# Splitting weights into two parts: the low part by an accumulating transfer, three units ahead, 64-byte tile offsets

## The chip, the cores and the metric

The kernel runs on one core of a Trainium2 chip. The metric is the time of one execution on the device in microseconds (us), the lower the better; a figure for a kernel is the median of its runs. The core has TensorE (PE, its weight loads PEld), VectorE (DVE), ScalarE (ACT), GpSimd (POOL) and the sync engine (SP, which here only issues DMAs), all in order, each with its own instruction stream, and 16 DMA engines that all queues share.

## The reference, cut to what matters

A decoder trunk of two layers on 512 tokens of width 1024, all in float32. Layer 0 mixes tokens by a chunked spatial gate, layer 1 by an attention with forget gates; a gated MLP with a short causal convolution follows each.

```python
for i in range(DEPTH):                      # DEPTH = 2
    hn = rmsnorm(h, mix_norm_g[i])
    mix = gating(hn, w_in, ..., w_out)      # i = 0: (u * s) @ w_out
          attention(hn, w_qkvf, b_f, w_o)   # i = 1: 16 heads of 64
    h = h + mix
    hn = rmsnorm(h, ffn_norm_g[i])
    h = h + (silu(conv3(hn @ w_gate)) * (hn @ w_up)) @ w_down
return rmsnorm(h, final_norm_g)
```

Nearly all the work is in the products with weights: 23 million weights, 92 MB.

## The kernel before

Every float32 product is made of three. Each operand is split into a high part, rounded to the format that TensorE multiplies at full rate (float32r), and a low part, the exact rest; `triple` (L164) then issues high by high, high by low and low by high (L167 to L169) into one bank of PSUM.

The weights lie in memory as 176 units of 128 rows by 1024 float32 (512 KB). `unit` (L85) hands out the next unit, and lets `fetch` (L75) prepare one more behind it: a DMA on SP's queue into a tile `raw` (three of them), a cast on ACT to `whi` (L112), and a subtraction on DVE, raw minus whi, to `wlo` (L113). There are two tiles each of `whi` and `wlo`, so the cast of a unit waits until TensorE has read the unit two before it. One unit feeds 8 blocks, 24 matmuls of 128 by 128 by 512. `fetch` makes 171 units so; unit 0 is split in two halves by `split` in `build`, and the last four are split into tiles `x` in `last_down`.

The stages, in order, with the units that each uses: the v half of the gate (16, tokens stationary, `gemm_tm`), its u half (16, weights stationary, `gemm_fm`, with the mixing of chunks between), its output product (16), gate and up of MLP 0 (32, eight groups of four units, with the convolution and silu after each group), down (16), the attention's values (8), queries and keys (16, the heads' work woven between), its output (8), gate and up of MLP 1 (32), and the last down product (16, tokens stationary). In the four output and down products the activations are the tiles `z` (32 of them); in the others they are the tiles `x` (16).

After an output product `add_to_h` (L211) adds the residual on DVE, makes the next `x` on ACT and DVE, and squares on ACT; `norm_square` (L132) adds the squares up on POOL (L141). Beside these 28 additions POOL has the constants of the start and 16 copies in the attention.

A scheduler decides the order in which each engine's instructions stand, from the program's order and its own estimate of when each is ready. Tiles get their place in a partition of SBUF in the order in which their names first come up, one behind the other: `raw`, `whi`, `wlo`, `x`, `tmp` come before `mv` (statistics of the gate, 4 by 2 float32, 32 bytes); `R`, `pt`, `tc`, `z` and `hl` come after it.

At the start (L673 to L705) TensorE warms up with 9 small matmuls on `ones`; unit 0 and the first quarter of the activations are loaded in halves, unit 1 is fetched between the rest of `x`.

Of the kernel before, what the change touches and what calls it, by code (L numbers as in the profile page):

```python
# [8 lines left out]
F32 = mybir.dt.float32  # L9
F32R = mybir.dt.float32r  # L10
BF16 = mybir.dt.bfloat16
I32 = mybir.dt.int32
AF = mybir.ActivationFunctionType
# [3 lines left out]
P = 128  # L17
T = 512            # tokens
D = 1024
KD = D // P        # feature tiles of the model width  # L20
E = 2048           # gMLP width and FFN width
KE = E // P
G = 8              # spatial groups
NT = T // P        # token tiles
H = 16             # heads
# [4 lines left out]
LAG = 7            # blocks between the logits and the sums of values  # L30

# columns of the packed per-feature vectors
V_MIX = 0          # mix_norm_g, 2 layers x 8 tiles
V_FFN = 16         # ffn_norm_g, 2 x 8
V_CW = 32          # conv taps, 2 x 3 x 16
V_CB = 128         # conv bias, 2 x 16
V_LG = 160         # ln_g, 16
V_LB = 176         # ln_b, 16
NV = 192
NU = 176           # units of weights  # L40


class Trunk:
# [31 lines left out]
    def fetch(self):  # L75
        nc = self.nc
        raw = self.sb("raw", 3, [P, 1024])
        nc.sync.dma_start(out=raw, in_=self.ins["w"][self.iu])
        self.iu += 1
        hi = self.sb("whi", 2, [P, 1024], F32R)  # L80
        lo = self.sb("wlo", 2, [P, 1024], F32R)
        self.split(hi, lo, raw)
        self.ahead.append((hi, lo))

    def unit(self):  # L85
        """The next unit of weights, in two parts; the one after it is under way."""
        while len(self.ahead) < 2 and self.iu < NU - 4:
            self.fetch()
        return self.ahead.pop(0)

# [1 line left out]
    def rsqrt(self, src, n, scale, eps):  # L92
        """[P, n] -> 1/sqrt(src*scale + eps): a first guess from the exponent, then Newton."""
        nc = self.nc
        ms, y, t = self.small(n), self.small(n), self.small(n)
        nc.vector.tensor_scalar(out=ms, in0=src, scalar1=scale, scalar2=eps, op0=ALU.mult, op1=ALU.add)
        nc.vector.tensor_scalar(out=y.bitcast(I32), in0=ms.bitcast(I32), scalar1=-0.5, scalar2=float(0x5F3759DF),
                                op0=ALU.mult, op1=ALU.add)
        for _ in range(3):
            self.newton(y, ms, t)  # L100
        return y

    def newton(self, y, ms, t):
        """y towards 1/sqrt(ms)."""
        nc = self.nc
        nc.vector.tensor_tensor(out=t, in0=y, in1=y, op=ALU.mult)
        nc.vector.scalar_tensor_tensor(out=t, in0=t, scalar=-0.5, in1=ms, op0=ALU.mult, op1=ALU.mult)
        nc.vector.scalar_tensor_tensor(out=y, in0=t, scalar=1.5, in1=y, op0=ALU.add, op1=ALU.mult)
# [6 lines left out]
    def norm_split(self, k, gcol, parts=1):  # L115
        """Operand parts of h*g for feature tile k."""
        nc = self.nc
        if k == 0:
            self.acc, self.xh, self.xl = None, [], []
        h = self.h[k]  # L120
        g = self.vec[:, gcol + k : gcol + k + 1]
        xh = self.sb("x", 16, [P, T], F32R)
        xl = self.sb("x", 16, [P, T], F32R)
        for q in range(parts):
            c = slice(q * T // parts, (q + 1) * T // parts)
            nc.scalar.activation(out=xh[:, c], in_=h[:, c], func=AF.Copy, scale=g)
            nc.vector.scalar_tensor_tensor(out=xl[:, c], in0=h[:, c], scalar=g, in1=xh[:, c].bitcast(F32),
                                           op0=ALU.mult, op1=ALU.subtract)
        self.xh.append(xh)
        self.xl.append(xl)  # L130

    def norm_square(self, k):  # L132
        """Feature tile k's share of the sum of squares."""
        nc = self.nc
        if self.acc is None:
            self.acc = self.tmp()
            nc.scalar.activation(out=self.acc, in_=self.h[k], func=AF.Square)
        else:
            sq = self.tmp()
            nc.scalar.activation(out=sq, in_=self.h[k], func=AF.Square)  # L140
            nc.gpsimd.tensor_tensor(out=self.acc, in0=self.acc, in1=sq, op=ALU.add)  # L141

    def norm_end(self):
        """r4[:, i]: 1/rms of token i*128+p.  R: the same along the free axis, on every partition."""
        nc = self.nc
        pt = self.ps("a")
        for i in range(NT):
            nc.tensor.matmul(pt[:, i : i + 1], self.acc[:, i * P : (i + 1) * P], self.ones[:, 0:1], start=True, stop=True)
        self.r4 = self.rsqrt(pt[:, 0:NT], NT, 1.0 / D, RMS_EPS)
        dg = self.tmp()  # L150
        for i in range(NT):
            nc.vector.tensor_scalar(out=dg[:, i * P : (i + 1) * P], in0=self.ident, scalar1=self.r4[:, i : i + 1],
                                    scalar2=None, op0=ALU.mult)
        self.dg = dg
# [9 lines left out]
    def triple(self, out, a, b, start, stop):  # L164
        """a*b to float32's accuracy from the exact parts of a and b."""
# [5 lines left out]
    def gemm_fm(self, o, nk, groups, evac, each=None, banks0=None):  # L171
        """Feature-major: four 128-feature tiles a group, weights stationary.  Yields after every 128x128 block."""
# [15 lines left out]
    def gemm_tm(self, o, nk, groups, evac, each=None):  # L188
        """Token-major: four token tiles a group of 512 features, tokens stationary."""
# [21 lines left out]
    def add_to_h(self, gcol):  # L211
        """Evacuation of an output product: the residual, then the next norm's operand."""
# [10 lines left out]
    def gmlp(self):  # L223
# [3 lines left out]
        mv = self.sb("mv", 1, [P, NT, 2])  # L227
# [38 lines left out]
        def mix(c):  # L266
            """The mixed chunks of feature tile c, with the norm's scale and shift and the spatial bias."""
# [42 lines left out]
    def spatial(self):  # L310
        """Causal spatial weights, transposed: [s, g, t], with their sums over s on every partition."""
# [46 lines left out]
    def fox(self):  # L358
# [4 lines left out]
        # the parts of the gates' weights side by side  # L363
# [44 lines left out]
        # Blocks of products fill the tensor engine's waits in the attention: logits of one head beside  # L408
        # the transposes and sums of the one before it.
# [20 lines left out]
    def gates(self):  # L430
        """Logs of the forget gates, [token, head]."""
# [14 lines left out]
        # log sigmoid z = min(z, 0) - log(1 + e^-|z|);  log(1 + e^-|z|) = 2 atanh s,  s = (1 - th)/(3 + th),  th = tanh(|z|/2)  # L446
# [15 lines left out]
    def running_sums(self):  # L462
        """Running sums of the logs, [head, token], in two parts, and negated: four rows a head beside the parts of
        q and of k: cum, cum, 1, 1 and 1, 1, -cum, -cum."""
# [29 lines left out]
    def stack_q(self, p, pq, st):  # L494
        """Operands of the logits of heads 2p and 2p+1: the parts of q and k, stacked along the contraction."""
# [22 lines left out]
    def attend(self, slot):  # L518
        """Logits of one block; some blocks behind them the transposes, and behind those the sums of values."""
# [9 lines left out]
    OFF = (0, 128, 384, 768)   # where the rows of a query block begin in a head's tile of probabilities  # L529

    def logits(self, h, qi):
        """Softmax's numerators of query block qi, and the diagonal of its normalizers' inverses."""
# [18 lines left out]
    def turn(self, h, kb):  # L551
        """Probabilities of key block kb, transposed and normalized, in two parts."""
# [8 lines left out]
        hl = self.sb("hl", 3, [P, 1024], F32R)  # L561
# [27 lines left out]
    def last_down(self):  # L589
        """Token-major down projection with the residual, then the final norm."""  # L590
# [13 lines left out]
        def finish(i, parts):  # L604
            # 1/rms from a square root and one step of Newton's
# [18 lines left out]
        for g in range(2):  # L624
            # a token tile's columns, in two parts where the norm of the last tile waits for them
# [22 lines left out]
        # the last quarter token tile by token tile, so that only the last tile's norm is left at the end  # L648
        last = []
        for kp in range(half, KE // 2):  # L650
            raw = self.sb("raw", 3, [P, 1024])
# [13 lines left out]
    def build(self):  # L665
        nc, tc = self.nc, self.tc
        with tc.tile_pool(name="sb", bufs=1) as self.pool, \
# [3 lines left out]
            # the activation table and the tensor engine's clock get ready while the first loads run  # L671
# [9 lines left out]
            raw = self.sb("raw", 3, [P, 1024])  # L681
            hi, lo = self.sb("whi", 2, [P, 1024], F32R), self.sb("wlo", 2, [P, 1024], F32R)
# [53 lines left out]
def blocks(w):  # L736
    """[K, 512*n] -> units of two 128-row tiles by 512 columns, group by group."""
# [5 lines left out]
def qk_blocks(w):  # L743
    """q and k columns of a pair of heads beside each other, four 128-row tiles a unit."""
# [49 lines left out]
```

## Time and profile before

| | us |
|---|---|
| three runs | 1111.95, 1113.28, 1115.22 |
| median | 1113.28 |
| span of the profiled execution | 1110.7 |
| TensorE busy in it | 1098.0 (99%) |
| DVE, ACT, POOL busy | 618.5, 443.5, 66.4 |
| granted TensorE clock, mean | 0.998 |

The profile is one execution on the chip, its times counted from the span's start. The median of the runs is 2.57 us above the profiled span. A matmul's recorded time overlaps that of its neighbours, since they are pipelined; its pace is read from the distance of two starts, or from how often a unit's buffers are released.

### The profile page before, as it was taken

Reading aid. Unit: us, or ns where it says so; the run is one execution under the profiler, and the core shown is the slowest. Engines: PE = TensorE matmul, PEld = TensorE weight load, DVE = VectorE, ACT = ScalarE, POOL = GpSimd, SP = SyncE. Lnnn points to the kernel's source line nnn. Section 1 sums busy time; section 2 is a strip of 40 time slices with the busy share of each in tenths; the row PEclk is TensorE's granted clock in tenths of the full one; section 3 lists DMA queues with packets and bytes.
Section 4 is the critical chain, followed back from the end, with each engine's and each line's share of the span. In section 5 each row is a group of like instructions: output and inputs, shape, how many; then the busy total and the mean of one; then the engine's idle time right before and its main releaser. Section 6 shows DMA issues by size and latency. Waiting matters only on the chain. (4 is left out here: it accounts for less than half of the span.)

```text
span 1110.7 us, 13297 instructions
## 1 busy us (share of the span) xinstructions
PE 1098.0 (99%) x5210; PEld 905.7 (82%) x5210; DVE 618.5 (56%) x1007; ACT 443.5 (40%) x706; POOL 66.4 (6%) x62
## 2 busy tenths in 40 slices
PE   8999999999999999999999999999999999999997
PEld 6878888888888888888888788888878888888886
DVE  6435765533556655624264688888665656644232
ACT  5332333332334333423142566776542434332222
POOL 6000000000200000001020000000021000000000
PEclk9999999999999999999999999999999999999999
DMA  7322222223222222222222212111122222222222
GB/s 245 103 78 98 91 76 95 76 95 95 95 95 95 94 95 95 95 96 94 95 95 82 79 40 62 58 40 58 62 90 95 95 96 95 95 95 94 96 77 76
DMA packets 28959, 99.47 MB, mean 90 GB/s; under 512 B 3488, under 2 KB 4256, under 8 KB 28896
## 3 DMA queue, kind: packets, MB, share of 16 engines
q1 hardware_dynamic: 28752, 98.52, 26.9%
q8 instruction: 41, 0.67, 0.2%
q14 instruction: 22, 0.18, 0.1%
q10 hardware_dynamic: 144, 0.10, 0.0%
HBM read 96.12 MB, written 2.10 MB: 88 GB/s over the span
## 5 line engine op out<-in xcount | busy, mean ns | idle before, releaser
L113 DVE TENSOR_TENSOR wlo<-raw,whi 128x1024 fp32r<-128x1024 f32 (+1 forms) x173 | 218.8, 1266 | 389.8 <-ACT whi L112 377.4
L112 ACT CAST whi<-raw 128x1024 fp32r<-128x1024 f32 (+1 forms) x173 | 180.7, 1045 | 467.0 <-PE psg L168 124.2
L167 PE MATMUL psg<-x,whi 128*128 128x512 f32 x336 | 136.7, 407 | 0.0
L169 PE MATMUL psg<-x,wlo 128*128 128x512 f32 x336 | 131.3, 391 | 0.0
L168 PE MATMUL psg<-x,whi 128*128 128x512 f32 x336 | 130.8, 389 | 0.0
L167 PE MATMUL pss<-x,whi 128*128 128x512 f32 x208 | 81.9, 394 | 0.0
L169 PE MATMUL pss<-x,wlo 128*128 128x512 f32 x208 | 81.0, 390 | 0.0
L168 PE MATMUL pss<-x,whi 128*128 128x512 f32 x208 | 80.9, 389 | 0.0
L169 PEld LDWEIGHTS psg<-x,wlo 128*128 128x128 f32 x336 | 63.1, 188 | 13.8
L167 PEld LDWEIGHTS psg<-x,whi 128*128 128x128 f32 x336 | 63.9, 190 | 11.1 <-issue 0.2
L168 PEld LDWEIGHTS psg<-x,whi 128*128 128x128 f32 x336 | 63.3, 189 | 11.2 <-issue 0.2
L141 POOL TENSOR_TENSOR tmp<-tmp,tmp 128x512 f32<-128x512 f32 x28 | 46.3, 1655 | 408.4 <-ACT tmp L140 406.9
L167 PE MATMUL psg<-z,whi 128*128 128x512 f32 x128 | 51.1, 401 | 0.0
L168 PE MATMUL psg<-z,whi 128*128 128x512 f32 x128 | 50.6, 395 | 0.0
L169 PE MATMUL psg<-z,wlo 128*128 128x512 f32 x128 | 50.6, 395 | 0.0
L559 PE MATMUL psa<-tmp,pt 128*128 128x128 f32 x320 | 47.4, 278 | 0.2 <-DVE hl L113 0.2
L168 PEld LDWEIGHTS pss<-x,whi 128*128 128x128 f32 x208 | 39.1, 188 | 8.2 <-issue 0.2
L169 PEld LDWEIGHTS pss<-x,wlo 128*128 128x128 f32 x208 | 39.0, 188 | 8.2
L547 ACT ACTIVATE pt<-pss,sm 128x128 f32<-128x128 f32 (+1 forms) x64 | 33.7, 527 | 30.1 <-DVE sm L546 29.7
L167 PEld LDWEIGHTS pss<-x,whi 128*128 128x128 f32 x208 | 39.1, 188 | 8.1 <-issue 0.2
L559 PEld LDWEIGHTS psa<-tmp,pt 128*128 128x128 f32 x320 | 43.1, 191 | 2.9 <-DVE hl L113 1.3
L167 PE MATMUL psa<-x,whi 128*128 128x512 f32 x112 | 44.2, 394 | 0.0
(283 smaller groups left out, 2279.2 us busy)
## 6 DMA issues: line engine op xcount, KB each, us to landing
raw<-w SPq DMA_DIRECT2D x175, 512.0 KB
out<-v SPq DMA_DIRECT2D x8, 256.0 KB
h<-x SPq DMA_DIRECT2D x3, 512.0 KB
raw<-w SPq DMA_DIRECT2D x2, 256.0 KB
h<-x SPq DMA_DIRECT2D x4, 128.0 KB
pt<-ws SPq DMA_DIRECT2D x1, 512.0 KB
pt<-bs SPq DMA_DIRECT2D x1, 512.0 KB
z<-cum SPq DMA_DIRECT2D x32, 8.0 KB
```

What stands on the lines that cost most here:

```text
L112: nc.scalar.copy(out=hi, in_=src)
L113: nc.vector.tensor_tensor(out=lo, in0=src, in1=hi.bitcast(F32), op=ALU.subtract)
L141: nc.gpsimd.tensor_tensor(out=self.acc, in0=self.acc, in1=sq, op=ALU.add)
L167: self.nc.tensor.matmul(out, ah, bh, start=start, stop=False)
L168: self.nc.tensor.matmul(out, ah, bl, start=False, stop=False)
L169: self.nc.tensor.matmul(out, al, bh, start=False, stop=stop)
L547: nc.scalar.activation(out=pr[:, self.OFF[qi] : self.OFF[qi] + w], in_=s[:, 0:w], func=AF.Exp, bias=nm, accum_out=sm)
L559: nc.tensor.matmul(pt[:, (qi - kb) * P : (qi - kb + 1) * P], pr[:, o : o + P], dg[:, qi * P : (qi + 1) * P], start=True, stop=True)
```

## The change

`split_by_dma` takes the place of `split` in `fetch`. ACT casts `raw` to `whi` as before, then writes minus `whi` into `wlo` (L89), and a DMA from POOL's queue (L90) reads the same unit of weights from memory again and adds it onto what stands in `wlo`. `raw` is free after the cast. `unit` keeps three units in the making where it kept two: `whi` and `wlo` have three tiles each, `raw` two where it had three, and `hl` (the transposed probabilities) two where it had three. `mv` takes 64 bytes where it took 32. All comments and docstrings are gone, with no effect on the program. Line numbers are 7 higher behind `fetch`.

```diff
     def fetch(self):
         nc = self.nc
-        raw = self.sb("raw", 3, [P, 1024])
+        raw = self.sb("raw", 2, [P, 1024])
         nc.sync.dma_start(out=raw, in_=self.ins["w"][self.iu])
         self.iu += 1
-        hi = self.sb("whi", 2, [P, 1024], F32R)
-        lo = self.sb("wlo", 2, [P, 1024], F32R)
-        self.split(hi, lo, raw)
+        hi = self.sb("whi", 3, [P, 1024], F32R)
+        lo = self.sb("wlo", 3, [P, 1024], F32R)
+        self.split_by_dma(hi, lo, raw, self.ins["w"][self.iu - 1])
         self.ahead.append((hi, lo))
 
+    def split_by_dma(self, hi, lo, raw, src):
+
+        nc = self.nc
+        nc.scalar.copy(out=hi, in_=raw)
+        nc.scalar.activation(out=lo, in_=hi.bitcast(F32), func=AF.Copy, scale=-1.0)
+        nc.gpsimd.dma_start(out=lo, in_=src, accum_op=ALU.add)
+
     def unit(self):
-        while len(self.ahead) < 2 and self.iu < NU - 4:
+        while len(self.ahead) < 3 and self.iu < NU - 4:
             self.fetch()
         return self.ahead.pop(0)
...
-        mv = self.sb("mv", 1, [P, NT, 2])
+        mv = self.sb("mv", 1, [P, NT, 4])[:, :, 0:2]
...
-        hl = self.sb("hl", 3, [P, 1024], F32R)
+        hl = self.sb("hl", 2, [P, 1024], F32R)
...
-            raw = self.sb("raw", 3, [P, 1024])
+            raw = self.sb("raw", 2, [P, 1024])
...
-            hi, lo = self.sb("whi", 2, [P, 1024], F32R), self.sb("wlo", 2, [P, 1024], F32R)
+            hi, lo = self.sb("whi", 3, [P, 1024], F32R), self.sb("wlo", 3, [P, 1024], F32R)
```

In the built programs the first `z` tile lies at byte 149,280 of a partition before (32 above a multiple of 64) and at 153,408 now (a multiple of 64); `R`, `pt`, `tc` and `hl` likewise lay 32 above one and lie on one now. `raw`, `whi`, `wlo`, `x` and `tmp` lie on multiples of 64 in both.

Three places in the order of instructions. First POOL at the start, before; `tmp` are the squares and their sum, `ident`, `fold` and `mask` constants, `pt_513` the spatial weights:

```order
L141 TENSOR_TENSOR tmp_139<-tmp_139,tmp_147 128x512
L141 TENSOR_TENSOR tmp_139<-tmp_139,tmp_150 128x512
L141 TENSOR_TENSOR tmp_139<-tmp_139,tmp_153 128x512
L141 TENSOR_TENSOR tmp_139<-tmp_139,tmp_156 128x512
L709 MEMSET tmp_166 128x128
L710 AFFINE_SELECT tmp_166<-tmp_166 128x128
L715 CAST maskb_173<-tmp_166 128x128
L141 TENSOR_TENSOR tmp_139<-tmp_139,tmp_159 128x512
L317 AFFINE_SELECT pt_513<-pt_513 128x1024
```

The same place now; `wlo_118`, `wlo_201` and `wlo_232` belong to units 1, 2 and 3:

```order
L148 TENSOR_TENSOR tmp_140<-tmp_140,tmp_148 128x512
L90 DMA wlo_118<-w 128x1024
L148 TENSOR_TENSOR tmp_140<-tmp_140,tmp_151 128x512
L148 TENSOR_TENSOR tmp_140<-tmp_140,tmp_154 128x512
L148 TENSOR_TENSOR tmp_140<-tmp_140,tmp_157 128x512
L716 MEMSET tmp_167 128x128
L717 AFFINE_SELECT tmp_167<-tmp_167 128x128
L722 CAST maskb_174<-tmp_167 128x128
L148 TENSOR_TENSOR tmp_140<-tmp_140,tmp_160 128x512
L324 AFFINE_SELECT pt_529<-pt_529 128x1024
L90 DMA wlo_201<-w 128x1024
L90 DMA wlo_232<-w 128x1024
```

The transfer for unit 1 stands behind the third addition that is shown as the first row here, and that for unit 2 behind all the additions, the mask and the masking of the spatial weights.

Second, TensorE at the first block of unit 1, before, with what each waits for:

```order
L167 MATMUL psg_193<-whi_117,x_107 128x512 [waits Activation_49]
L167 MATMUL psg_194<-whi_117,x_107 128x512
L167 MATMUL pss_195<-whi_117,x_107 128x512
L167 MATMUL pss_196<-whi_117,x_107 128x512
L168 MATMUL psg_193<-wlo_118,x_107 128x512 [waits DVE_49]
```

And now:

```order
L174 MATMUL psg_194<-whi_117,x_107 128x512 [waits Activation_49]
L174 MATMUL psg_195<-whi_117,x_107 128x512
L174 MATMUL pss_196<-whi_117,x_107 128x512
L174 MATMUL pss_197<-whi_117,x_107 128x512
L175 MATMUL psg_194<-wlo_118,x_107 128x512 [waits DMASW0_49]
```

The order of the matmuls is the same; the fifth waits for the transfer in place of DVE.

Third, ACT around the end of a group of MLP 0, before; `v` holds the convolution's values, `z` its split result:

```order
L112 CAST whi_3114<-raw_3112 128x1024
L344 ACTIVATE v_3142<-v_3142,vec_79 128x512 x2
L112 CAST whi_3171<-raw_3169 128x1024
L347 ACTIVATE v_3142<-v_3142 128x512 x2
L112 CAST z_3150<-v_3142 128x512
L112 CAST z_3161<-v_3142 128x512
L112 CAST whi_3201<-raw_3199 128x1024
```

And now:

```order
L89 ACTIVATE wlo_2442<-whi_2441 128x1024
L351 ACTIVATE v_2470<-v_2470,vec_79 128x512 x2
L354 ACTIVATE v_2470<-v_2470 128x512
L88 CAST whi_2499<-raw_2497 128x1024
L89 ACTIVATE wlo_2500<-whi_2499 128x1024
L354 ACTIVATE v_2470<-v_2470 128x512
L119 CAST z_2478<-v_2470 128x512
L119 CAST z_2489<-v_2470 128x512
L88 CAST whi_2530<-raw_2528 128x1024
```

The negation stands right behind each cast of a unit, and that pair stands between the two silus of the group.

## Rows read from the trace of the kernel before

**Rows 1.** Page, part 1: busy us (share of the span) and instructions

```profile
PE 1098.0 (99%) x5210; PEld 905.7 (82%) x5210; DVE 618.5 (56%) x1007; ACT 443.5 (40%) x706; POOL 66.4 (6%) x62
```

**Rows 2.** Waits of TensorE: who waited for whom, total us, times, longest

```profile
PE psg L168 <- DVE wlo L113: 2.3, 2, 1.4
PE psa L169 <- DVE wlo L113: 1.0, 1, 1.0
```

**Rows 3.** Groups by line: busy us, mean ns, idle before, releaser

```profile
L113 DVE TENSOR_TENSOR wlo<-raw,whi 128x1024 fp32r<-128x1024 f32 (+1 forms) x173 | 218.8, 1266 | 389.8 <-ACT whi L112 377.4 <-PE psb L272 12.3
L112 ACT CAST whi<-raw 128x1024 fp32r<-128x1024 f32 (+1 forms) x173 | 180.7, 1045 | 467.0 <-PE psg L168 124.2 <-PE pss L168 118.5 <-PE psb L168 104.4
L126 ACT ACTIVATE x<-h,vec 128x512 fp32r<-128x512 f32 (+1 forms) x34 | 23.2, 689 | 11.7 <-DVE h L216 11.7
L112 ACT CAST z<-v 128x512 fp32r<-128x512 f32 x32 | 19.4, 621 | 11.5 <-DVE v L349 11.5
```

**Rows 4.** Timeline of ACT in MLP 0: start, us, instruction, idle before and releaser

```profile
326.80 1.05 ACT L112 CAST whi<-raw 128x1024 fp32r<-128x1024 f32 x1 [1.37 <-PE psb L168]
...
348.60 1.05 ACT L112 CAST whi<-raw 128x1024 fp32r<-128x1024 f32 x1 [4.43 <-PE pss L168]
...
370.36 1.05 ACT L112 CAST whi<-raw 128x1024 fp32r<-128x1024 f32 x1 [4.43 <-PE psg L168]
```

**Rows 5.** Timeline of ACT in the gate's output product

```profile
258.67 1.05 ACT L112 CAST whi<-raw 128x1024 fp32r<-128x1024 f32 x1 [4.51 <-PE pss L168]
...
286.67 1.05 ACT L112 CAST whi<-raw 128x1024 fp32r<-128x1024 f32 x1 [4.55 <-PE pss L168]
```

**Rows 6.** Page, part 3: DMA queue, packets, MB, share of 16 engines' span

```profile
q1 hardware_dynamic: 28752, 98.52, 26.9%
```

**Rows 7.** Timeline of SP's queue late in the last product: issue of a load

```profile
1058.73 0.33 SPq L652 DMA_DIRECT2D raw<-w  x1
```

**Rows 8.** Timeline of ACT there: the first instruction that uses that load

```profile
1062.02 1.14 ACT L112 CAST x<-raw 128x512 fp32r<-128x512 f32 x2 [4.58 <-DMA raw<-w]
```

**Rows 9.** Timeline of POOL at the start

```profile
15.40 6.91 POOL L141 TENSOR_TENSOR tmp<-tmp,tmp 128x512 f32<-128x512 f32 x4
22.26 0.20 POOL L709 MEMSET tmp<- 128x128 f32 x1
22.53 1.02 POOL L710 TENSOR_SCALAR_AFFINE_SELECT tmp<-tmp 128x128 f32<-128x128 f32 x1
23.61 0.29 POOL L715 CAST maskb<-tmp 128x128 bf16<-128x128 f32 x1
23.87 1.29 POOL L141 TENSOR_TENSOR tmp<-tmp,tmp 128x512 f32<-128x512 f32 x1
25.11 1.09 POOL L317 TENSOR_SCALAR_AFFINE_SELECT pt<-pt 128x1024 f32<-128x1024 f32 x1
```

**Rows 10.** Timeline of TensorE at the start

```profile
1.06 3.61 PE L676 MATMUL psb<-ones 128*128 128x128 f32 x18 [1.06 <-POOL ones L670]
...
14.05 0.50 PE L168 MATMUL psg<-wlo,x 128*128 128x512 f32 x1 [0.87 <-DVE wlo L113]
...
19.17 0.61 PE L167 MATMUL pss<-whi,x 128*128 128x512 f32 x2
21.22 0.50 PE L168 MATMUL psg<-wlo,x 128*128 128x512 f32 x1 [1.44 <-DVE wlo L113]
...
25.89 0.39 PE L167 MATMUL psg<-whi,x 128*128 128x512 f32 x1
```

**Rows 11.** Chain that ended last, in order of time: start, us, what

```profile
1009.14 1.79 PE psg L634 x16
```

**Rows 12.** Timeline of POOL at the end of the gate's output product

```profile
291.00 6.94 POOL L141 TENSOR_TENSOR tmp<-tmp,tmp 128x512 f32<-128x512 f32 x4 [38.24 <-ACT tmp L140]
```

**Rows 13.** Two stretches, at the start and in the attention: busy PE, PEld, DVE, ACT, POOL; clock, DMA share, GB/s

```profile
10.00:15.00 5.00, 3.71 (x15) 2.43 (x14) 4.82 (x5) 5.00 (x9) 4.92 (x6) 1.00 0.94 370
700.00:725.00 25.00, 25.00 (x151) 21.33 (x151) 21.23 (x52) 18.15 (x42) 1.23 (x2) 1.00 0.14 45
```

More of the change, by code (lines that the diff above doesn't have):

```diff
@@ L680, in build @@
             nc.scalar.dma_start(out=self.vec, in_=self.ins["vec"])
-            raw = self.sb("raw", 3, [P, 1024])
-            hi, lo = self.sb("whi", 2, [P, 1024], F32R), self.sb("wlo", 2, [P, 1024], F32R)
+            raw = self.sb("raw", 2, [P, 1024])
+            hi, lo = self.sb("whi", 3, [P, 1024], F32R), self.sb("wlo", 3, [P, 1024], F32R)
             for j in range(2):
```

## Prediction, before the run

> **What bounds the kernel now.** The page's busy times come first [rows 1]: TensorE is busy 1098.0 of 1110.7 us, DVE 618.5, ACT 443.5, POOL 66.4. A busy TensorE need not be at its best pace, so the list of its waits is read next [rows 2]. In the whole span it waits on DVE's `wlo` for 2.3 + 1.0 = 3.3 us, 2.3 of them in two waits at the start (0.87 and 1.44) [rows 10]. That is all that a faster split can give back by waits. The 1226 ns or so that DVE spends on each unit [rows 3] lie beside TensorE's work; taking some 210 us off DVE is worth nothing by itself.
>
> What remains is TensorE's pace, read from how often ACT's cast of a unit is released, each time by the last reading of an older unit. In MLP 0 eight units pass from 326.80 to 370.36, 5.445 us each [rows 4]. In the gate's output product five pass from 258.67 to 286.67, 5.60 us each [rows 5]. Both are 24 matmuls with 512 columns, and in both TensorE never rests; one reads `x`, the other `z`. So `z` costs 0.155 us a unit, 6.5 ns a matmul. Other engines are no reason: ACT is idle 4.5 us between those casts.
>
> **The change, part by part.** *The steady state.* Three tiles of `whi` and `wlo` give the making of a unit two units of time: a cast starts when a unit is released, its result is wanted 2 x 5.445 us later, and `wlo` two matmuls (0.45) after that: 11.35 us. Into this must go the cast, 1.05 us [rows 4]; the negation, which the trace doesn't show, between 1.05 (a cast) and 1.17 (by 689 against 621 ns for a scaled write and a cast of 512 columns [rows 3]), I take 1.17; some 0.2 for handovers; and the transfer with POOL's work for it. That leaves it 8.9 us. ACT gets 171 x 1.17 = 200 us more, where it is idle 4.4 us a unit [rows 4]; in the attention it has 25 - 18.15 = 6.85 us free of 25 and two to three units come by [rows 13], so I cost that at nothing; without that cover it would be some 1.2 us a unit. At the end of an MLP group the order puts cast and negation between the two silus, after work that starts when the group's first banks are done; the cast is not pushed behind the whole group's finish, and I cost that at nothing too.
>
> *The transfer's landing.* No row shows an accumulating DMA or one from POOL. From below: it moves no less than a plain load, which takes from issue to first use 1062.02 - 1058.73 = 3.3 us [rows 7, 8]. From above: the room of 8.9 us, past which the prediction is another one (a rival below). The plain load's engine time is 26.9% of 1110.7 us = 299 us [rows 6] for 98.52 MB, which is 188 units' worth, so 1.59 us a unit. If reading the target and writing it add 1.59 and POOL's issue 1, the landing is 3.3 + 1.6 + 1 = 5.9; I take **6 us**, nearer to the plain load than to the room.
>
> *DMA engines.* Two plain loads' worth for the transfer and one for `raw` make 4.8 us of 5.445: it fits, though tight. Reading the source, reading the target and writing it one after the other make 6.4: it doesn't fit. I take the first, because the row of a plain load already holds one reading and one writing. The Trainium skill bears on that: *Collectives: The Full Stack*, section on the bandwidth ceiling, says that adding in the DMA costs no cycles of its own but needs two source reads, so that such transfers ran at half the rate of copies. By that page the engine time would be 3.2 us, the same as the value taken; no row here shows it.
>
> *The start.* This is where the change costs. Unit 1's transfer stands on POOL behind an addition, unit 2's behind three more additions, the mask and the masking of the spatial weights. POOL's four additions take 6.91 us from 15.40, 1.73 each [rows 9], so unit 1's is issued at 17.1 at the earliest and lands at 23.1; TensorE wanted it at about 13.2 and got it at 14.05 [rows 10]. For unit 2 add 1.0 for POOL's issue (estimated), 3 x 1.73 for the additions, 1.6 for memset, selection and cast (22.26 to 23.87), 1.29 and 1.09 [rows 9]: issued at 27.3, landed at 33.3. TensorE has then finished unit 1 (23.1 + 4.67, the time from 21.22 to unit 3's first matmul at 25.89 [rows 10]) and waits. Unit 2's `wlo` came at 21.22 before, so the start costs **12.1 us** (9.4 with a landing of 3.3, 15.0 with 8.9). Unit 3's transfer is issued right behind and is wanted 5 us after unit 2's, so it costs nothing more.
>
> *Pace after a rest.* The 18 warm-up records take 3.61 us [rows 10], the 16 of the same shape in the last product 1.79 [rows 11]; at the later pace 18 would take 2.0, so a start from rest loses 1.6. The rest before unit 1 (10 us) is paid inside the second wait; the one before unit 2 (some 4) may be followed by such a slow stretch. I take half, **0.8 us**, with 0 to 3.2 as bounds. The skill has a rule here (*TensorE: Matmul & The Clock Gate*, part 1): an idle array falls to 1.2 GHz and regains 2.4 GHz by work. Every stretch asked of the trace shows the granted clock at 1.00 [rows 13], the upper level, so no row confirms it; by it the whole bound of 3.2 would be likely.
>
> *Additions before a transfer.* After each output product three or four additions stand before a transfer on POOL, six places. The last of them ends at 291.00 + 6.94 = 297.94 [rows 12], 5.7 us after the unit's release at 286.67 + 5.60; with 6 us for the landing `wlo` comes at 11.7, 0.35 late. Over six places I take **1 us** (0 where DVE's lighter load speeds the additions up, 6 where the landing takes 1 us more).
>
> *What goes.* TensorE's mid-span wait on DVE, [rows 2]: **-1.0 us** (those at the start are in the start's sum). `hl` with two tiles adds no wait: the sums of an older block precede the new block's transposes on TensorE.
>
> *The offsets.* `z` moves from 32 above a multiple of 64 bytes to a multiple, where `x` lies. If that offset is what slows `z`, its products come down to the pace of `x`: 16 + 16 + 8 + 16 = 56 units x 0.155 = **-8.7 us**. For it: both places of the pace fit, and it is the difference that the change itself undoes. Against it: `z` also lies higher in memory, which stays. I take it in whole; the other end is 0. In the attention a little more may come or go (2 us either way), taken as 0.
>
> *Sum:* 12.1 + 0.8 + 1.0 - 1.0 - 8.7 = +4.2 on the profiled 1110.7, 1114.9; the runs' median stands 2.57 above the span, so **1117.5 us**, with 1112 to 1123 as this case's own range.
>
> **The rivals.** *Not slower: the transfer lands like a plain load.* The start then costs 9.4, TensorE resumes at full pace, no addition matters: 9.4 - 1.0 - 8.7 = -0.3, and with 2 us in the attention **1111 us**. It decides from a landing below about 3.6 us, or if the additions at the start run quicker than 1.73. The row of the plain load speaks for it; POOL's issue and the second reading against.
>
> *The offset isn't what slows `z`*: nothing is gained, 1117.5 + 8.7 = **1126 us**. The upper place of `z` in memory speaks for it. This is the case in which the 64 bytes don't do what they are put there for.
>
> *The transfer cannot keep pace.* Past 3.85 us of engine time a unit (5.445 - 1.59), or past 8.9 us of landing, every unit outside the attention waits. With three plain trips, 6.4 against 5.445, 0.92 x 146 units = 134, and the time is about **1250 us** (1140 to 1300 for less and more). DMA engines that read and write in one pass speak against it, the missing row for it.
>
> **How the numbers follow.** Chances: forecast 0.45, not slower 0.15, offset without effect 0.18, pace 0.22. A measurement of this kernel tells about 0.3% from no change, 3.3 us: 1109.9 to 1116.6. The forecast's own range lies two fifths in that (0.19) and else above (0.26); of the rival that is not slower 0.09 lies within and 0.06 below; the other two are slower. So faster 0.06, same 0.28, slower 0.66. The range of 8 in 10 leaves out some 0.07 below 1110 and some 0.13 above 1200, where the slow end of the pace rival lies.
>
> **What would show it.** In the profile after: TensorE's two waits at the start on the transfer, to 23 and 33 us, unit 3 at about 38; no wait of TensorE on `wlo` in the MLPs; units of the output and down products at 5.445 us (5.60 if the offset does nothing); DMA share near 0.9 in the MLPs (4.8 of 5.445); POOL's additions at the start still near 1.7. If TensorE waits on the transfer in every unit, the landing or the DMA engines' time is wrong; if the start costs under 9 us, the landing or POOL's order of cost is.

## The result, and the profile after

| | before | after |
|---|---|---|
| median of the runs, us | 1114.0 (4 runs) | 1120.6 (4 runs, 1118.9 to 1122.0) |
| span of the profiled execution | 1110.7 | 1116.7 |
| granted TensorE clock, mean | 0.998 | 0.993 |
| ratio after / before | | 1.0063, 95% interval 1.0047 to 1.0078 |

The changed kernel is slower by some 6.6 us. The predicted 1117.5 is 3.1 us below, on the right side; two terms of its sum were off by some 4 us, in opposite directions, and a third by 2.

The page of the changed kernel, parts 1 and 2 (busy time; the busy share of the DMA engines in 40 slices of the span, in tenths):

```profile
PE 1096.0 (98%) x5210; PEld 908.0 (81%) x5210; DVE 414.8 (37%) x836; ACT 619.9 (56%) x877; POOL 210.3 (19%) x233
...
DMA  8788767788778888887885844434468888886852
```

Against [rows 1], DVE has lost 203.7 us, ACT has won 176.4 and POOL 143.9, and TensorE is as busy as before. The DMA engines are busy eight tenths of the time in the MLPs. The waits of TensorE (us in total, times, longest) answer to [rows 2]:

```profile
PE psg L175 <- DMA wlo<-w: 9.3, 1, 9.3
PE psa L176 <- DMA wlo<-w: 3.2, 1, 3.2
```

There are two waits on `wlo` in the whole span, one at the start and one at 823 us in the attention's output product, and none in the MLPs. Parts 3, 5 and 6 of the page give what a transfer costs (queue: packets, MB, share of 16 engines; group: busy us, mean ns; issues: KB, us from issue to landing):

```profile
q0 software_dynamic: 24624, 89.66, 47.1%
q1 hardware_dynamic: 28752, 98.52, 25.1%
...
L90 POOL DMA_DIRECT2D wlo<-w x171 | 150.1, 879 | 782.0 <-ACT wlo L89 731.1
L89 ACT ACTIVATE wlo<-whi 128x1024 fp32r<-128x1024 f32 x171 | 181.1, 1060 | 4.3
...
wlo<-w POOLq DMA_DIRECT2D x171, 512.0 KB, 6.0
```

A transfer takes 47.1% of 1116.7 us / 171 = 3.08 us of the 16 engines, a plain load 25.1% of it / 188 = 1.49; POOL is held 0.88 us by the issue, the landing comes 6.0 us after it, and the negation takes 1.06.

**Where the time went**, from the starts of the same matmul in the two traces (unit 3's first matmul stood at 25.89 [rows 10] and stands at 34.32 below):

| stretch | change, us |
|---|---|
| start, to unit 3's first matmul | +8.4 |
| gate's v and u halves | -0.4 |
| gate's output product (units of 5.60 [rows 5] come down to 5.494, by ACT's casts at 260.13 and 287.60) | -1.7 |
| MLP 0, gate and up | 0.0 |
| MLP 0, down | -1.7 |
| attention, before its output product | -0.2 |
| attention's output: the wait of 3.2, DVE's of 1.0 gone, pace | +1.8 |
| MLP 1, gate and up | 0.0 |
| last product | -0.4 |
| sum | +5.8 (spans: +6.0) |

*The start.* The timeline of POOL in the changed kernel (start, us, instruction, idle before and releaser):

```profile
12.39 0.29 POOL L720 CAST identb<-ident 128x128 bf16<-128x128 f32 x1
...
13.08 1.26 POOL L148 TENSOR_TENSOR tmp<-tmp,tmp 128x512 f32<-128x512 f32 x1
14.29 0.99 POOL L90 DMA_DIRECT2D wlo<-w  x1
15.04 4.91 POOL L148 TENSOR_TENSOR tmp<-tmp,tmp 128x512 f32<-128x512 f32 x3
...
23.22 1.74 POOL L90 DMA_DIRECT2D wlo<-w  x2
```

The timeline of TensorE there:

```profile
21.97 0.80 PE L175 MATMUL psg<-wlo,x 128*128 128x512 f32 x1 [9.27 <-DMA wlo<-w]
...
23.42 0.63 PE L175 MATMUL psg<-wlo,x 128*128 128x512 f32 x1
23.85 0.63 PE L176 MATMUL psg<-whi,x 128*128 128x512 f32 x1
...
29.79 0.39 PE L175 MATMUL psg<-wlo,x 128*128 128x512 f32 x1
...
34.32 0.39 PE L174 MATMUL psg<-whi,x 128*128 128x512 f32 x1
```

Unit 1's transfer is issued at 14.29 behind an addition, and TensorE goes on with it at 21.97, 7.7 us later, while the loads of the start keep the DMA engines at a share of 0.99. Behind the rest matmuls start 0.43 us apart in place of 0.227. The stretches show the clock (length; busy PE, PEld, DVE, ACT, POOL; clock, DMA share, GB/s):

```profile
15.00:20.00 5.00, 0.00 (x0) 0.00 (x0) 5.00 (x3) 5.00 (x8) 4.84 (x5) 0.65 0.99 250
20.00:25.00 5.00, 3.03 (x7) 2.45 (x8) 0.49 (x1) 1.24 (x2) 4.82 (x7) 0.50 0.84 264
25.00:30.00 5.00, 5.00 (x19) 3.98 (x19) 0.00 (x0) 0.92 (x1) 0.00 (x0) 0.83 0.99 182
```

0.50 is the level of 1.2 GHz, and before the change each of these stretches showed 1.00, as the one in [rows 13] does. The Trainium skill (*TensorE: Matmul & The Clock Gate*, Part 1) says that an idle array falls to that level and works its way back; these rows agree. In the trace the transfer of unit 2 has landed at 28.86, and TensorE first reads it at 29.79: there is no second wait, and TensorE comes 0.9 us later than the transfer.

*The wait at 823 us.* The timeline of ACT ahead of it:

```profile
815.10 0.71 ACT L133 ACTIVATE x<-h,vec 128x512 fp32r<-128x512 f32 x1
815.71 1.04 ACT L88 CAST whi<-raw 128x1024 fp32r<-128x1024 f32 x1
816.77 1.06 ACT L89 ACTIVATE wlo<-whi 128x1024 fp32r<-128x1024 f32 x1
```

That of POOL:

```profile
813.07 4.71 POOL L148 TENSOR_TENSOR tmp<-tmp,tmp 128x512 f32<-128x512 f32 x3 [3.42 <-ACT tmp L147]
818.25 0.89 POOL L90 DMA_DIRECT2D wlo<-w  x1 [0.47 <-ACT wlo L89]
```

And TensorE's matmul that waits:

```profile
826.86 0.51 PE L176 MATMUL psa<-z,wlo 128*128 128x512 f32 x1 [3.19 <-DMA wlo<-w]
```

TensorE had read the unit's old buffers by 812, but on ACT the cast stands behind the evacuation of four `x` tiles and starts at 815.71; the negation ends at 817.83, POOL's additions at 817.78. POOL still waits 0.47 us for ACT, and the transfer goes out at 818.25, some 6.3 us behind the release. At the other five places where a transfer stands behind additions it leaves right behind the additions, lands 5.6 to 5.8 us later, and TensorE does not wait. Here it lands 8.6 us later, while the next transfer, issued at 820.28, and loads are under way. With a landing of 5.8 it would have been 0.4 us late, so 2.8 of the 3.2 us come from the landing. The clock does not fall behind this rest of 3.2 us.

### The profile page after: what moved, and what is told of

It reads as the page before. It is cut to its first block, busy times and chain, and to the rows that moved or that the text cites. A ratio compares the mean times of both kernels' runs of the same rounds, so it can differ in the third digit from the quotient of the medians.

```text
span 1116.7 us, 13647 instructions
## 1 busy us (share of the span) xinstructions
PE 1096.0 (98%) x5210; PEld 908.0 (81%) x5210; DVE 414.8 (37%) x836; ACT 619.9 (56%) x877; POOL 210.3 (19%) x233
## 3 DMA queue, kind: packets, MB, share of 16 engines
q0 software_dynamic: 24624, 89.66, 47.1%
q1 hardware_dynamic: 28752, 98.52, 25.1%
## 4 chain that ended last, share of the span: by engine, by line
PE 95%; DMA 2%; ACT 1%; POOL 1%; DVE 1%; issue 0%; SPq 0%; DVEq 0%; POOLq 0%; ACTq 0%
PE psg L174 12%; PE psg L176 11%; PE psg L175 11%; PE pss L176 8%; PE pss L174 8%; PE pss L175 8%; PE psa L174 4%; PE psa L176 4%; PE psa L175 4%; PE psb L174 4%; PE psb L175 4%; PE psb L176 4%; PE psa L566 3%; DMA wlo<-w 1%; PE pss L550 1%; PE psb L580 1%
## 5 line engine op out<-in xcount | busy, mean ns | idle before, releaser
L88 ACT CAST whi<-raw 128x1024 fp32r<-128x1024 f32 x171 | 179.2, 1049 | 351.9 <-PE psg L175 99.0
L90 POOL DMA_DIRECT2D wlo<-w x171 | 150.1, 879 | 782.0 <-ACT wlo L89 731.1
L89 ACT ACTIVATE wlo<-whi 128x1024 fp32r<-128x1024 f32 x171 | 181.1, 1060 | 4.3
L566 PE MATMUL psa<-tmp,pt 128*128 128x128 f32 x320 | 47.1, 278 | 0.3 <-DVE hl L120 0.3
```

The costliest lines, as they stand in the source:

```text
L88: nc.scalar.copy(out=hi, in_=raw)
L89: nc.scalar.activation(out=lo, in_=hi.bitcast(F32), func=AF.Copy, scale=-1.0)
L90: nc.gpsimd.dma_start(out=lo, in_=src, accum_op=ALU.add)
L566: nc.tensor.matmul(pt[:, (qi - kb) * P : (qi - kb + 1) * P], pr[:, o : o + P], dg[:, qi * P : (qi + 1) * P], start=True, stop=True)
```

## The experiments

Twelve kernels, each against the kernel before on the same chip (its median there 1113.8 to 1115.2).

**The offset alone** (the kernel before with one line):

```diff
-        mv = self.sb("mv", 1, [P, NT, 2])
+        mv = self.sb("mv", 1, [P, NT, 4])[:, :, 0:2]
```

> The kernel before with one edit, 64 bytes for mv in place of 32, so that R, pt, tc, z and hl move from 32 to 64 above a multiple of 128 bytes; the making of the weights stays as it was. Theory (the traces' ledger): the offset takes 0.107 us off a unit in the gate's output and MLP 0's down product, 1.7 us each, half of that in the attention's output, under 0.5 in the last product, about 5 us in all: 1109 us, with units of the gate's output at 5.49. Rival A, the recorded term in whole: 5.445 us a unit in all 56 units, -8.7, 1105.3. Rival B: the offset does nothing by itself and the faster units of the changed kernel come from DVE's lighter load: 1114.

Measured: 1108.7, ratio 0.9959 (0.9947 to 0.9971), 5.0 us less than before. The offset pays without any transfer, but not in whole. The timeline of ACT, two casts five units apart in the gate's output, where `z` moves, and two casts four units apart in the last product, where `z` is stationary:

```profile
257.82 1.05 ACT L112 CAST whi<-raw 128x1024 fp32r<-128x1024 f32 x1 [4.39 <-PE pss L168]
...
285.29 1.05 ACT L112 CAST whi<-raw 128x1024 fp32r<-128x1024 f32 x1 [4.44 <-PE pss L168]
...
1024.56 1.05 ACT L112 CAST whi<-raw 128x1024 fp32r<-128x1024 f32 x1 [4.51 <-PE psg L169]
...
1046.96 1.05 ACT L112 CAST whi<-raw 128x1024 fp32r<-128x1024 f32 x1 [4.55 <-PE psg L169]
```

Units of the gate's output take 27.47 / 5 = 5.494 us, those of the last product still 22.40 / 4 = 5.60.

**The change without its offset** (the line undone in the changed kernel):

> The changed kernel with mv at 32 bytes again: the accumulating transfers and three units in the making, tiles where they lay (32 above a multiple of 64). Theory: the change without its offset loses what the offset gave, about 5 us: 1125.6, with units of the gate's output at 5.60, start and the wait in the attention's output as in the changed kernel. Rival A: 1129.3, where the offset is worth 8.7. Rival B: 1120.6, where it is worth nothing and DVE's lighter load gave the pace of z.

Measured: 1125.8, ratio 1.0115 (1.0101 to 1.0130). The transfer and the third unit cost some 12 us, the offset gives 5 back; with the first run the two parts add up.

**Is a multiple of 128 better?** (`[P, NT, 8]` in the kernel before)

> The kernel before with 128 bytes for mv, so that R, pt, tc, z and hl lie on multiples of 128 bytes, as raw, whi, wlo, x, tmp and v do. Theory: what is left of the slowness of z (5.49 against 5.445 us a unit, and 5.6 in the last product) is its place 64 above a multiple of 128; all 56 units come down to 5.445, 8.7 us less than the kernel before, 1105.3. Rival: a multiple of 64 is all that counts, the rest is that z lies higher in a partition or in the stationary role: like the run with 64 bytes, about 1109. A third: larger multiples do nothing more in the moving role but the last product, with z stationary, comes down by 16 x 0.155 = 2.5: 1106.5.

Measured: 1113.3, ratio 0.9999 (0.9991 to 1.0008). All three expectations failed. The tiles now lie on multiples of 64 and of 128 and the gain is gone: units take 5.576. So "a multiple of 64 bytes" is not what helps.

**Multiples of 512 and of 256** (`[P, NT, 16]` puts `z` on multiples of 512, `[P, NT, 32]` 256 above one):

> The kernel before with 256 bytes for mv: z lies on multiples of 2048 bytes (its first tile at 149,504), pt, R and tc on multiples of 512; x lies 1024 above a multiple of 2048. Theory, formed after the run with 128 bytes gave nothing: the pace of a product depends on how its two operands' addresses stand to each other modulo a larger power of two, since x (a multiple of 1024) and whi run at 226.7 ns a matmul while z at 288, 320 and 384 above a multiple of 512 takes 233.3, 229 and 232.5. Then all 56 units with z come to 5.44 us: 1113.8 - 8.7 = 1105. Rival: z is slow because it lies above 128 KB (or for the places of the single tiles), and only the 64 above 128 helps: 1113, units at 5.55 to 5.60.

> The kernel before with 512 bytes for mv: z's tiles lie 256 above a multiple of 512 (first tile at 149,760). Theory: a multiple of 256 is as good as one of 512, 1105. If the modulus is 512, it is slow like 128: about 1113, units of the gate's output at 5.55 to 5.60. Rival (only the bit of 64 counts, odd multiples of 64 being good): 1113 here and in the run with multiples of 512.

Measured: 1105.5, ratio 0.9924 (0.9906 to 0.9941), and 1108.0, ratio 0.9943 (0.9925 to 0.9961). In both traces every product with `z` runs at 226 to 227 ns a matmul, the last one too; the 2.5 us between the two medians are not in the traces (the profiled execution with 256 took 1105.2). The timeline of ACT in the gate's output, two casts five units apart, with multiples of 128:

```profile
257.80 1.05 ACT L112 CAST whi<-raw 128x1024 fp32r<-128x1024 f32 x1 [4.49 <-PE pss L168]
...
285.68 1.05 ACT L112 CAST whi<-raw 128x1024 fp32r<-128x1024 f32 x1 [4.53 <-PE pss L168]
```

The same with multiples of 512:

```profile
257.95 1.06 ACT L112 CAST whi<-raw 128x1024 fp32r<-128x1024 f32 x1 [4.34 <-PE pss L168]
...
285.15 1.05 ACT L112 CAST whi<-raw 128x1024 fp32r<-128x1024 f32 x1 [4.38 <-PE pss L168]
```

And in the run that follows below, with 512 and everything shifted by 32:

```profile
260.35 1.05 ACT L112 CAST whi<-raw 128x1024 fp32r<-128x1024 f32 x1 [4.34 <-PE pss L168]
...
287.55 1.05 ACT L112 CAST whi<-raw 128x1024 fp32r<-128x1024 f32 x1 [4.38 <-PE pss L168]
```

27.88 / 5 = 5.576, 27.20 / 5 = 5.44 and 27.20 / 5 = 5.44; before it was 28.00 / 5 [rows 5].

**The address itself, or the distance of the two operands?** (the run with 512, and `vec` 32 bytes longer, so that weights, `x` and `z` all move by 32)

```diff
-            self.vec = self.sb("vec", 1, [P, NV])
+            self.vec = self.sb("vec", 1, [P, NV + 8])[:, 0:NV]
```

> The kernel with multiples of 512 for z (1105.5), with 32 bytes more for vec, so that all that lies behind it, raw, whi, wlo, x, tmp, v, pt, z and hl, is 32 above a multiple of 256. Theory: what slows a matmul is the address of an operand itself, so now the products of x are slow too: some 4300 matmuls of 512 columns by 6.6 ns = +28 us, 1134, with units of MLP 0 at 5.6 us. Rival: only how the two operands lie to each other counts; z stands to whi as before, and the time is 1105.5.

Measured: 1108.5 in one execution; its span is 2.3 us above the run with 512, all of it in the first 29 us, and every product with `z` stays at 226 to 227 ns. With all tiles 32 above a multiple of 64 nothing is slow. So the address itself does not count, but where `z` lies against the tiles ahead of it: 0 modulo 256 bytes is fast; 32, 64 and 128 are not. The runs move `z` against all those tiles at once (`raw`, `whi`, `wlo`, `x`, `tmp`); that it is the distance to the weights is argued from their being the other operand of these matmuls.

**The start split by DVE** (the changed kernel):

```diff
-        self.split_by_dma(hi, lo, raw, self.ins["w"][self.iu - 1])
+        if self.iu - 1 <= 4:
+            self.split(hi, lo, raw)
+        else:
+            self.split_by_dma(hi, lo, raw, self.ins["w"][self.iu - 1])
```

> The changed kernel, but units 1 to 4 are split by DVE as in the kernel before; from unit 5 on the transfer does it. Theory: the start is all that the late first transfer costs (9.3 us of wait and 10 matmuls at half pace, 8.4 in all by the starts of the same matmul), so 1120.6 - 8.4 = 1112.2, the granted clock stays at 1.00 in all stretches of the first 40 us, TensorE's waits there are 0.9 and 1.4 as before. Rival: unit 5's transfer is then the first and waits behind POOL's start; a wait of some 5 us moves to unit 5 and the time is about 1117.

Measured: 1114.3, 6.3 less than the changed kernel, its executions between 1110.7 and 1116.7. The profiled one took 1110.7; in its trace the same matmuls come 8.3 us earlier from the start on, the clock is at 1.00 in every stretch from 10 to 45 us, and TensorE's two waits on transfers, in the attention's output, are 2.0 and 0.5. So the start's cost is as thought; that most of its other executions lose some 4 us more is not seen in this trace.

**The start and the attention's output by DVE** (`if self.iu - 1 <= 4 or 120 <= self.iu - 1 < 128`):

> The changed kernel with units 1 to 4 and the eight units of the attention's output product (120 to 127) split by DVE, all others by the transfer. Theory: the change consists of the start, +8.3, the late unit in the attention's output, +3.2, and the offset, -5.0; without the first two the rest is the offset alone: 1120.6 - 8.3 - 3.2 = 1109.1, the same as the kernel before with 64 bytes (1108.7), and no wait of TensorE on the transfer over 0.5 us. Rival, after the run with units 1 to 4 alone came at 1114.3 (6.3 less, and its executions spread over 1110.7 to 1116.7): waits on transfers elsewhere take some 2 us that one profile does not show: 1111 to 1112.

Measured: 1109.6, ratio 0.9965 (0.9953 to 0.9977), and no wait of TensorE on a transfer is left. That is 0.9 above the offset alone. It accounts for the change: start, one late unit, offset; 159 units by transfer are worth nothing, neither way. The 4.7 us below the run before, for waits of 2.5 us there, suggest that these waits are what varies between executions; the granted clock of the single executions fits (0.993 to 0.998 in the run before, 0.996 to 0.999 here), but no trace shows it.

**No rest at the start** (38 matmuls that nobody reads, in TensorE's wait for unit 1; the edit, cut to them; it also issues by hand the four matmuls that stand ahead of the wait):

```diff
...
+                    idle = self.ps("b")
+                    for _ in range(38):
+                        self.nc.tensor.matmul(idle, oh[2][:, 0:P], hi[:, 0:512], start=True, stop=True)
...
```

> The changed kernel, with 38 matmuls of 512 columns that nobody reads put into TensorE's wait for unit 1 (first high part by first x tile, into a bank that is free; 38 x 0.227 = 8.6 of the 9.3 us). The transfers stay as late as they are. Theory: half the pace behind the rest is a cost of its own, 10 matmuls at 0.427 in place of 0.227 and what follows, 2.0 to 2.2 us: TensorE rests 0.6 us, the clock stays at 1.00 in the stretch from 20 to 30 us, unit 2's first matmul comes 2 us earlier than 28.88, and the time is 1120.6 - 2.1 = 1118.5. Rival: the matmuls are slow because transfers and loads crowd the memory then; the pace stays at 0.43 and the time at 1120.6.

Measured: 1120.5, as without them. POOL's transfers for units 2 and 3 in it, from the timeline of POOL:

```profile
24.01 1.74 POOL L90 DMA_DIRECT2D wlo<-w  x2
```

TensorE:

```profile
13.82 8.80 PE L212 MATMUL psb<-whi,x 128*128 128x512 f32 x38
22.91 0.50 PE L218 MATMUL psg<-wlo,x 128*128 128x512 f32 x1 [0.29 <-DMA wlo<-w]
...
29.78 0.50 PE L175 MATMUL psg<-wlo,x 128*128 128x512 f32 x1 [1.81 <-DMA wlo<-w]
```

The clock stays at 1.00 in all stretches and the matmuls at 0.227 us, as the theory said; crowded memory, the rival, falls. But the time gained is waited away: a second wait, of 1.8 us, appears for unit 2, whose transfer goes out at 24.01 (23.22 without the matmuls). What sets the start here is the landing of unit 2's transfer, 5.8 us behind its issue.

That the slow pace costs nothing does not follow. Two other things moved in this run: POOL's transfers go out 0.7 to 0.8 us later from the first on (14.96 against 14.29), and TensorE's order at unit 2 has one matmul ahead of the first that reads the transfer, where the changed kernel has four. In the changed kernel the 20 matmuls from 21.97 take 6.91 us, here those from 22.91 take 4.67: the slow pace takes 2.2 us. Of these 1.3 would have been waited for unit 2's transfer (landed at 28.86, read at 29.79), and 0.9 are lost. Medians of four executions don't show 0.9 us.

**Two units in the making** (the changed kernel with two tiles of `whi` and `wlo` and a lookahead of two):

> The changed kernel with two tiles of whi and wlo and two units in the making, as before the change; the transfers stay. Theory: the chain of cast 1.05, negation 1.06, handovers 0.3 and landing 6.0 is 8.4 us, and with two tiles a unit has 5.44 + 0.45 = 5.9: two units take 8.4 + 4.99 = 13.4, 6.7 each, 1.25 more in some 140 units, about 1120.6 + 175 = 1295, with a wait of TensorE on the transfer in nearly every second or every unit of the MLPs. Rival: where nothing competes the landing is like a plain load's 3.3, chain 5.7, and two units would do: 1121.

Measured: 1397.6 in one execution. Part 1 of its page:

```profile
PE 1194.3 (86%) x5210; PEld 952.1 (68%) x5210; DVE 415.0 (30%) x836; ACT 619.7 (44%) x877; POOL 206.2 (15%) x233
```

TensorE's waits on the transfer (us in total, times, longest):

```profile
PE psg L176 <- DMA wlo<-w: 58.9, 28, 3.2
PE psa L176 <- DMA wlo<-w: 51.2, 25, 3.4
PE pss L176 <- DMA wlo<-w: 37.3, 20, 3.0
PE psg L175 <- DMA wlo<-w: 19.8, 7, 9.4
PE pss L175 <- DMA wlo<-w: 11.8, 7, 2.7
PE psa L175 <- DMA wlo<-w: 11.0, 4, 3.1
```

The waits sum to 190.0 us, 177.5 more than in the changed kernel, where the chain of 8.4 us against a room of 5.9 gave 175. Another 98 us are TensorE's busy time, 1194.3 against 1096.0, at a granted clock of 0.938 in the mean: behind some rests of 2 to 3 us the next 6 to 14 matmuls run at half pace, behind others hardly one. Some 330 matmuls of 512 columns start 0.40 to 0.45 us after one another, which makes 65 of the 98; where the rest of the 98 lies is open. The expectation had left this out. The third unit is what makes the transfer possible.

**One more copy for each of units 32 to 111:**

```diff
+        if 32 <= self.iu - 1 < 112:
+            again = self.sb("hl", 2, [P, 1024], F32R)
+            nc.sync.dma_start(out=again.bitcast(F32), in_=hi.bitcast(F32))
```

> The changed kernel with one more DMA of 512 KB for each of units 32 to 111 (a copy of the high part within the core's memory, which nobody reads), issued by SP. Theory: the transfer takes 3.1 us of the 16 engines and the load 1.6, 4.7 of 5.44 us a unit, so it fits with 14% to spare; a further 1.6 makes 6.3, which doesn't fit: the units in this range take 6.3 or more in place of 5.44, TensorE waits on the transfer 0.8 us or more a unit and its clock falls after some waits, so +70 to +120 us: 1190 to 1240, with the DMA share at 1.0 there. Rival: the engines' busy shares include waiting and hide room; the copy fits and the time stays at 1121.

Measured: 1131.9 in one execution, 11 us above the changed kernel's median. By the starts of the same matmul its trace is 13.0 us behind the changed kernel's: 2.5 come at the start, before any copy, 8.0 in the stages with copies, 2.5 in the attention's output, behind them. The stretch from 340 to 440 us (columns as above):

```profile
340.00:440.00 100.00, 99.42 (x436) 81.38 (x435) 37.93 (x58) 56.40 (x65) 15.78 (x19) 1.00 1.01 288
```

Its queues, and the transfer's landing:

```profile
q0 software_dynamic: 2692, 9.83, 53.3%
q1 hardware_dynamic: 5190, 18.90, 47.7%
...
wlo<-w POOLq DMA_DIRECT2D x19, 512.0 KB, 8.0
```

The engines are full, the landing grows to 8.0 us, and TensorE waits 0.6 of 100 us. The theory erred in adding the shares up: with 18.75 units here the transfer takes 53.3 / 18.75 = 2.84 us, less than the 3.08 at a lower load, and a plain one 47.7 / 36.05 = 1.32 (loads and copies taken together). The packets of the traces say why the copy fits. In this stretch the median packet of 4 KB takes 159 ns if it is plain and 328 if it adds, the same in the changed kernel; the means are higher by the slower packets. A unit is 128 such packets, 8 for each of the 16 engines: 8 x 0.328 + 2 x 8 x 0.159 = 5.17 us of a unit's 5.44. The 8 us in 80 units make 0.1 a unit, so the copy nearly fits.

**DVE's split, three units, multiples of 512** (the changed kernel's buffers, `split` for all units, `[P, NT, 16]`):

> The changed kernel with the split of all units back on DVE (no negation, no transfer), three units in the making, raw and hl with two tiles as in the change, and 256 bytes for mv, so that z lies on multiples of 2048. Theory: the alignment gives 8.5 us as in the run with multiples of 512, and the third unit can give at most the mid-span wait of TensorE on DVE, 1.0 us: 1104.5 (1104 to 1106). Rival: DVE with a unit more at the start crowds the first units' low parts or the x tiles there, up to 2 us more: 1107.5.

Measured: 1106.1, ratio 0.9920 (0.9908 to 0.9933). The mid-span wait on DVE is gone (the attention's output is 1.5 us shorter than with 512 alone), and the start is 1.9 us longer. The third unit is worth nothing to DVE's split. This kernel and the kernel before with 512, at 1105.5, are the fastest, 9.1 and 8.5 us below the kernel before.

## Why the prediction came out as it did

- *The bound.* Right (the 1226 ns named there for DVE's split of a unit is not in its row, which has 1266, a mean over two shapes; nothing hangs on it). 203.7 us of DVE's work are gone, and where neither start, nor late unit, nor `z` plays a part, matmuls start as far apart as before.
- *The steady state.* Right: negation 1.06 (1.17 taken), landing 6.0 (6), engine time 3.08 (3.2), no wait in the MLPs; with two units the room fails by the amount that the same chain gives. The rule of the Trainium skill on adding in the DMA (*Collectives: The Full Stack*, section on the bandwidth ceiling) is half the rate of a copy. The traces agree: 3.08 to 1.49. The case of a transfer that cannot keep pace, with 0.22, was too likely: even a third copy a unit nearly fits.
- *The start*, 12.1 + 0.8: mechanism right, size off, +8.4, under the 9 us that the prediction itself had named as a sign of a wrong landing or of wrong costs on POOL. It was POOL: the mis-sized terms are its issue times, 14.29 and 23.22 where 17.1 and 27.3 were taken; POOL's own issue, put at 1 without a row, took 0.99 and 0.88. Unit 1's landing took more, 7.7 for 6. I had taken POOL's durations from a trace in which DVE works beside it. Before, POOL's cast and copy took

```profile
12.87 1.28 POOL L713 CAST identb<-ident 128x128 bf16<-128x128 f32 x1
14.10 0.65 POOL L719 COPY fold<-ident 32x16 f32<-32x16 f32 x1
```

  while DVE made unit 1's `wlo` and then `x`:

```profile
11.96 2.04 DVE L113 TENSOR_TENSOR wlo<-raw,whi 128x1024 fp32r<-128x1024 f32 x1 [0.18 <-ACT whi L112]
13.92 5.01 DVE L127 SCALAR_TENSOR_TENSOR x<-h,vec,x 128x512 fp32r<-128x512 f32 x4
```

  In the changed kernel DVE has no subtraction there and idles until 13.57:

```profile
13.57 6.92 DVE L134 SCALAR_TENSOR_TENSOR x<-h,vec,x 128x512 fp32r<-128x512 f32 x4 [2.27 <-ACT x L133]
```

  There `identb` takes 0.29 at 12.39. POOL's additions do the same: 1.26 and 1.29 beside an idle DVE, at 20.97 now and at 23.87 before [rows 9], 1.64 and 1.73 beside a busy one. The Trainium skill (*SBUF — State Buffer*, section on who interferes with whom) says that a DVE instruction with two inputs in SBUF contends with a POOL instruction that reads SBUF; the traces agree. No run changed DVE's work there alone; as far as these rows go, the change takes away the cause of the durations on which its cost was reckoned.
- *Pace after a rest*, 0.8: the clock did fall, but behind the first rest. The prediction had that slow stretch paid inside a second wait and took 0.8 for a slow stretch behind the second; there was no second wait, and of the 2.2 us that the slow pace behind the first took, 0.9 were lost. That 0.8 and 0.9 are so near is luck.
- *Additions before a transfer*, +1.0 over six places: five places cost nothing, one cost 3.2. The first part of the step came near: there the transfer leaves some 6.3 us behind the release, where the additions alone had made 5.7. The step looked at POOL alone; ACT's cast came 3.7 us late there, so that its negation ended only when the additions did. The mis-sized term is the landing, 8.6 where 6 was taken.
- *What goes*, -1.0: right; the wait on DVE is gone.
- *The offsets*, -8.7: the step failed. 5.0 came. The step held the place of `z` against a multiple of 64, since that is what the change alters, and took the whole difference to `x` as its price. The runs show another rule, the distance to the weights modulo 256; the change only moved it from 32 to 64. Nearly the whole difference was there to be had: with a distance of 0 the medians give 8.5, the stages with `z` in the profiled execution 7.4.

The cost of the start was put 4.5 too high, the gain of the offset 3.7 too high, and the late unit 2.2 too low: the errors cancel to 1.4 of the 1.8 us by which the sum, 4.2, fell short of the spans' 6.0. The forecast held for this reason, not because each term did.

## What to carry to other kernels

Try to let the two operands of a matmul lie a multiple of 256 bytes apart in a partition: here, with float32r and 512 columns, it gave 0.8% for one line, more than all else in this study. A transfer that takes over an engine's work pays only where that engine is waited for; what it costs is read at the places where its issuing queue is busy or the unit late (here the start and the end of a product), not in the steady state alone. And durations at a place where an edit removes a neighbour's work are better taken from a place where that neighbour is idle.

## What the runs showed of the hardware

- The pace of 128 by 128 by 512 matmuls in float32r depends on how far `z` lies from the tiles ahead of it, the weights among them, modulo 256 bytes: 0 gives 226.7 ns, 32 gives 233.3, 64 gives 229 with `z` moving (232, 226 and 229 in turn over the three products) and 233.3 with `z` stationary, 128 gives 232 to 233. Shifting all of them by 32 changes nothing. Other distances were not tried, nor why it is so.
- An accumulating transfer of 512 KB took 6.0 us from issue to landing (7.7 and 8.6 at the two places where TensorE waited), 3.08 us of the 16 engines and 0.88 of POOL; a plain load took 1.49 of the engines.
- The engines' busy share is no sum of fixed costs: at a share of 1.01 the transfer took 2.84 us of them, over the whole changed kernel 3.08; the median packet took the same time in both, 328 ns.
- A rest of 9.3 us is followed by matmuls 0.43 us apart; with 38 idle matmuls in it the clock stays at 1.00. With two units in the making, and 91 waits on the transfer, half pace cost some 65 of the 279 us that the time grew by.
